# The first adaLN modulation computed feature tile by feature tile, with the first input projection k-outer inside it

## Chip, cores and metric

One core of one Trainium2 chip runs the kernel. The metric is the device time of one execution in microseconds (us); of several executions the median is given.

## What is computed

The reference runs two layers of a trunk on two groups of tokens, 512 latent tokens and 128 context tokens, with shared weights and 1024 features. Each layer modulates a normalised input, projects it to 8208 columns that feed three mixers and their gates, merges the branches, and ends with an MLP:

```python
mod_ctx = (jax.nn.silu(c_ctx) @ w_mod[l] + b_mod[l])[None, None, :]
mod_lat = (jax.nn.silu(c) @ w_mod[l] + b_mod[l])[:, None, :]
...
sh1, sc1, g1, sh2, sc2, g2 = jnp.split(mod, 6, axis=-1)
h = rmsnorm(x, lp['norm1']) * (1 + sc1) + sh1
proj = h @ lp['w_in'] + lp['b_in']
(da_q, da_k, da_v, ml_q, ml_k, ml_v, ml_o, ml_g,
 na_q, na_k, na_v, merge) = jnp.split(proj, np.cumsum(SPLIT_SIZES)[:-1].tolist(), axis=-1)
...
x = x + g1 * (merged @ lp['w_out'])
h2 = rmsnorm(x, lp['norm2']) * (1 + sc2) + sh2
u = jnp.square(jax.nn.relu(h2 @ lp['w_ff1'] + lp['b_ff1']))
x = x + g2 * (u @ lp['w_ff2'] + lp['b_ff2'])
```

The change lies in the first layer's `h` and the first two blocks of its `proj`: the columns `ml_v`, and the 16 gate columns `ml_g`.

## The kernel before

All 640 tokens stay on the chip, with features on the partitions: eight feature tiles `xT[k]` of 128 features by 640 tokens. Every float32 product is made of three float32r products, so each weight block and each activation is split into a rounded part `hi` and a rest `lo` (`split`, lines 215 to 218: ScalarE casts, VectorE subtracts). A weight block is 1 MB: 1024 features by 256 columns. `w_raw` asks for it on SP's queue (line 141), and there are two buffers. `gemm_b` (lines 200 to 213) makes 128 tokens by 256 columns: eight feature tiles times three matmuls, on lines 210, 211 and 212, which accumulate in one PSUM bank. `unit_b` does this for the five token tiles `t`; a unit's first step asks for the next unit's weights.

`start` (lines 1604 to 1664) is what comes ahead of the first unit. It asks for the eight feature tiles of x, sums their squares over the features (lines 1619 and 1621, then a matmul with ones, line 1636), takes 1/rms on GpSimd (line 1639), spreads it over the partitions with diagonal matrices and ones (lines 1643 and 1644), and multiplies it into x (line 1646). In between, `mod_first` (lines 278 to 299) computes the shift and scale of the first modulation, 2048 columns for the two conditioning vectors `cc3`. The 8 MB of weights `w_mod0` lie by input feature: tile k holds 128 input features by all 2048 columns. So each of the eight tiles adds to one PSUM bank, and the result exists only after the last tile. Four matmuls on line 287 write two rows each at partitions 0, 32, 64 and 96:

```python
for q in range(4):
    nc.tensor.matmul(ps[32 * q:32 * q + 2, :], self.cc3[:, :, k], raw[:, q * 512:(q + 1) * 512],
                     start=(k == 0), stop=(k == KD - 1))
```

Then the rows are copied (lines 291 and 292), transposed (line 295), added to the bias columns (line 299) and turned into a scale `A` and a shift `B` for each feature. Lines 1658 and 1660 apply them by token bank, (0, 256) and (256, 640), and split the result into the activations. The first unit's `gemm_b` follows: columns `ml_v` 0 to 255 with the 16 gate columns, 272 in all. Its evacuations (lines 604 and 610) feed the gate chain `ml_gates`, whose first step on TensorE is a transpose for each token tile (line 667). The second unit takes columns 256 to 511.

The order of instructions on each engine is set by a scheduling layer under the kernel's code, which moves an instruction ahead of others when it sees its inputs ready. What runs is that order, engine by engine, with semaphores; an engine executes its own instructions strictly one after the other.

Of the kernel before, what the change touches and what calls it, by code (L numbers as in the profile page):

```python
# [11 lines left out]
F32 = mybir.dt.float32  # L12
F32R = mybir.dt.float32r
AF = mybir.ActivationFunctionType
# [5 lines left out]
P = 128  # L20
# [5 lines left out]
TT = 5  # L26
# [60 lines left out]
class Builder:  # L87
# [190 lines left out]
    def mod_first(self, after):  # L278

        nc, I = self.nc, self.I  # L280
        ps = self.mm_ps()
        nc.vector.memset(ps, 0.0)
        for k in range(KD):
            raw = self.T(self.xp, [P, 2048], F32, "raw8", 6)
            nc.sync.dma_start(raw, I["w_mod0"][k])
            for q in range(4):
                nc.tensor.matmul(ps[32 * q:32 * q + 2, :], self.cc3[:, :, k], raw[:, q * 512:(q + 1) * 512],
                                 start=(k == 0), stop=(k == KD - 1))
            after(k)
        row = self.T(self.xp, [P, 512], F32, "modrow", 1)  # L290
        nc.vector.tensor_copy(row[:, :256], ps[:, :256])
        nc.scalar.copy(row[:, 256:], ps[:, 256:])
        tp = self.mm_ps()
        for j in range(4):
            nc.tensor.transpose(tp[:, j * P:(j + 1) * P], row[:, j * P:(j + 1) * P], self.ident)
        t4 = tp.rearrange("p (j q z) -> p j q z", j=4, q=4)
        jq = lambda x: x.rearrange("p (q j) -> p j q", q=4)
        for v in range(2):
            nc.vector.tensor_tensor(jq(self.modc[0][:, v, 0:16]), t4[:, :, :, v], jq(self.colv[0][1][:, 0:16]), op=ALU.add)

# [133 lines left out]
    def unit_b(self, c0, consume, extra=None):  # L434

        def prep():
            return self.w_bmode(self.in_blk(self.l, c0), extra=extra)

        def run(w):
            for t in range(TT):  # L440
                consume(t, self.gemm_b(w, self.act, t))
                yield
        return prep, run, None
# [1160 lines left out]
    def start(self):  # L1604

        tc, nc, I = self.tc, self.nc, self.I
        with tc.tile_pool(name="xp_in", bufs=1, reuse_waits="tile") as xp:
            self.xp = xp
            loads, fin = self.load_cols(0)
            self.xsrc = [I["x_sample"][0, t * P:(t + 1) * P] for t in range(4)] + [I["x_prompt"][0]]  # L1610
            xT = [self.hd() for _ in range(KD)]
            ws = []
            ones = self.T(xp, [P, P], F32, "ones", 1)
            nc.gpsimd.memset(ones, 1.0)
            acc = self.T(xp, [P, NT], F32, "acc", 1)
            for k in range(KD):
                nc.sync.dma_start(xT[k], I["xT"][:, k])
                sq = acc if k == 0 else self.T(xp, [P, NT], F32, "sq", 2)
                nc.scalar.activation(sq, xT[k], AF.Square)
                if k:  # L1620
                    nc.vector.tensor_tensor(acc, acc, sq, op=ALU.add)

            def after(k):
                if k == 1:
                    for o, i in loads:
                        nc.sync.dma_start(o, i)
                    fin()
                    normalize()
                if k == 4:
                    ws.append(self.first_w_in(0)())  # L1630

            def normalize():

                ps = self.t_ps()
                for t in range(TT):
                    nc.tensor.matmul(ps[:, 2 * t:2 * t + 2], acc[:, t * P:(t + 1) * P], ones[:, :2], start=True, stop=True)
                ss, r = self.st(5), self.st(5)
                nc.vector.tensor_scalar(ss, ps[:, 0:2 * TT:2], 1.0 / D, EPS, op0=ALU.mult, op1=ALU.add)
                nc.gpsimd.tensor_tensor(r, ss, self.mhalf[:, :TT], op=ALU.pow)
                rb = self.s_ps()  # L1640
                for t in range(TT):
                    dg = self.T(xp, [P, P], F32, "diag", 2)
                    nc.vector.tensor_scalar_mul(dg, self.ident, r[:, t:t + 1])
                    nc.tensor.matmul(rb[:, t * P:(t + 1) * P], ones, dg, start=True, stop=True)
                for k in range(KD):
                    nc.vector.tensor_tensor(xT[k], xT[k], rb[:, :NT], op=ALU.mult)
            self.mod_first(after)
            w, = ws
            A, B = self.mod_norm_cols(0, 0)
            act = [(self.act_slice(), self.act_slice()) for _ in range(KD)]  # L1650
            for a, b in BANKS:
                for k in range(KD):
                    x = xT[k]
                    for v, c0, c1 in ((0, a, min(b, NS)), (1, max(a, NS), b)):
                        if c0 >= c1:
                            continue
                        if a > 0 and v == 0 or a == 0 and k % 3 == 1:
                            nc.scalar.activation(x[:, c0:c1], x[:, c0:c1], AF.Identity, scale=A[:, v, k:k + 1], bias=B[:, v, k:k + 1])
                        else:
                            nc.vector.tensor_scalar(x[:, c0:c1], x[:, c0:c1], A[:, v, k:k + 1], B[:, v, k:k + 1],  # L1660
                                                    op0=ALU.mult, op1=ALU.add)
# [125 lines left out]
```

## Time and profile before

| what | us |
|---|---|
| median of 3 runs | 2491.88 |
| lowest and highest run | 2488.35 and 2492.19 |
| the profiled execution, its own time | 2490.52 |
| its span in the profile | 2488.7 |
| TensorE matmuls, busy | 2415.0 |
| VectorE, ScalarE, GpSimd, busy | 1523.0, 905.1, 640.9 |

The profiled execution is one run more, recorded by the hardware. Its span is 1.8 us shorter than its own time, which holds the launch as well. All times inside the trace count from the span's start. Busy shares are averages over the whole program; the stretch that the change touches is the first 60 us of it.

### The profile page before, as it was taken

The numbers are of one execution on the slowest core, as the hardware profiler recorded it, in microseconds if no ns is written. First come the engines' busy times: TensorE is split into PE (matmuls) and PEld (weight loads), VectorE is DVE, ScalarE is ACT, GpSimd is POOL, SyncE is SP. The second block draws the span as 40 slices with busy tenths as digits, with TensorE's granted clock in tenths as the row PEclk, the third lists the DMA queues.
The fourth block names the chain that finished last, engine by engine and source line by source line (L and its number), as shares of the span: only waits on it lengthen the run. The fifth ranks groups of instructions, "written<-read, shape, count | busy, mean of one in ns | idle before, by whom it ended". The sixth has DMA issues, their size and how long they took to land. (4 is left out here: it accounts for less than half of the span.)

```text
span 2488.7 us, 39544 instructions
## 1 busy us (share of the span) xinstructions
PE 2415.0 (97%) x15776; PEld 2266.3 (91%) x15776; DVE 1523.0 (61%) x2804; ACT 905.1 (36%) x1954; POOL 640.9 (26%) x701
## 2 busy tenths in 40 slices
PE   6999999999999999999999999999999999999998
PEld 4999999999998898999989999999989889999997
DVE  5557788566634899998565547674443464444444
ACT  4332354334433422223353334443443353322232
POOL 0122122233412233332021212222352312233301
PEclk8999999999999999999999999999999999999999
DMA  7323323333353334444332222223232722222221
GB/s 271 105 94 117 112 97 135 121 117 123 139 190 130 119 136 152 153 136 153 103 122 97 96 90 87 76 82 111 74 116 86 261 85 85 68 85 68 85 68 60
DMA packets 73706, 286.52 MB, mean 115 GB/s; under 512 B 9889, under 2 KB 21249, under 8 KB 49969
## 3 DMA queue, kind: packets, MB, share of 16 engines
q1 hardware_dynamic: 73520, 283.99, 33.3%
q8 instruction: 124, 2.03, 0.3%
q14 instruction: 62, 0.50, 0.1%
HBM read 257.60 MB, written 26.35 MB: 114 GB/s over the span
## 5 line engine op out<-in xcount | busy, mean ns | idle before, releaser
L191 PE MATMUL mm<-act,whi 128*128 128x384 f32 (+1 forms) x2176 | 699.4, 321 | 11.7 <-DVE act L503 3.4
L192 PE MATMUL mm<-act,whi 128*128 128x384 f32 (+1 forms) x2176 | 687.5, 316 | 0.0
L193 PE MATMUL mm<-act,wlo 128*128 128x384 f32 (+1 forms) x2176 | 686.0, 315 | 0.0
L217 ACT CAST whi<-raw 128x1024 fp32r<-128x1024 f32 x296 | 310.9, 1050 | 921.3 <-PE mm L192 439.3
L218 DVE TENSOR_TENSOR wlo<-raw,whi 128x1024 fp32r<-128x1024 f32 x296 | 383.8, 1297 | 381.3 <-ACT whi L217 327.2
L191 PEld LDWEIGHTS mm<-act,whi 128*128 128x128 f32 x2176 | 413.9, 190 | 17.5 <-issue 6.0
L192 PEld LDWEIGHTS mm<-act,whi 128*128 128x128 f32 x2176 | 414.3, 190 | 0.0
L193 PEld LDWEIGHTS mm<-act,wlo 128*128 128x128 f32 x2176 | 413.8, 190 | 0.0
L1535 POOL TENSOR_TENSOR x<-x,tmp 128x512 f32<-128x512 f32 x120 | 194.0, 1623 | 448.5 <-DVE tmp L1534 448.5
L210 PE MATMUL mm<-whi,act 128*128 128x256 f32 (+2 forms) x800 | 270.0, 338 | 0.0
L212 PE MATMUL mm<-whi,act 128*128 128x256 f32 (+2 forms) x800 | 267.1, 334 | 0.0
L211 PE MATMUL mm<-wlo,act 128*128 128x256 f32 (+2 forms) x800 | 266.4, 333 | 0.0
L323 DVE SCALAR_TENSOR_TENSOR macc<-raw,cc,macc 128x512 f32<-128x512 f32 x280 | 232.2, 874 | 20.0 <-DMA raw<-w_mod 19.6
L212 PEld LDWEIGHTS mm<-whi,act 128*128 128x128 f32 x800 | 152.0, 190 | 14.3
L211 PEld LDWEIGHTS mm<-wlo,act 128*128 128x128 f32 x800 | 152.1, 190 | 14.0
L210 PEld LDWEIGHTS mm<-whi,act 128*128 128x128 f32 x800 | 152.1, 190 | 14.0
L210 PE MATMUL t<-whi,act 128*128 128x512 f32 (+1 forms) x416 | 158.5, 381 | 1.7 <-ACT act L217 1.5
L211 PE MATMUL t<-wlo,act 128*128 128x512 f32 (+1 forms) x416 | 157.8, 379 | 0.0
L212 PE MATMUL t<-whi,act 128*128 128x512 f32 (+1 forms) x416 | 157.8, 379 | 0.0
L192 PE MATMUL t<-act,whi 128*128 128x256 f32 (+1 forms) x512 | 146.4, 286 | 0.0
L193 PE MATMUL t<-act,wlo 128*128 128x256 f32 (+1 forms) x512 | 146.4, 286 | 0.0
L191 PE MATMUL t<-act,whi 128*128 128x256 f32 (+1 forms) x512 | 146.2, 286 | 0.0
(286 smaller groups left out, 4168.6 us busy)
## 6 DMA issues: line engine op xcount, KB each, us to landing
raw<-w_in SPq DMA_DIRECT2D x64, 1024.0 KB
raw<-w_ff SPq DMA_DIRECT2D x64, 1024.0 KB
raw<-w_mod SPq DMA_DIRECT2D x48, 1024.0 KB
mgd<-act SPq DMA_DIRECT2D x32, 320.0 KB
act<-mgd SPq DMA_DIRECT2D x32, 320.0 KB
raw<-w_out SPq DMA_DIRECT2D x8, 1024.0 KB
gr<-gd SPq DMA_DIRECT2D x12, 512.0 KB
act<-rd SPq DMA_DIRECT2D x16, 320.0 KB
```

Of the source, the lines that this page charges most:

```text
L191: nc.tensor.matmul(o, wh, ah, start=(k == 0), stop=False)
L192: nc.tensor.matmul(o, wh, al, start=False, stop=False)
L193: nc.tensor.matmul(o, wl, ah, start=False, stop=(k == nk - 1))
L210: nc.tensor.matmul(o, ah, wh, start=(first and k == 0), stop=False)
L211: nc.tensor.matmul(o, ah, wlo, start=False, stop=False)
L212: nc.tensor.matmul(o, al, wh, start=False, stop=(last and k == nk - 1))
L217: self.nc.scalar.copy(hi, src)
L218: self.nc.vector.tensor_tensor(lo, src, hi.bitcast(F32), op=ALU.subtract)
L323: nc.vector.scalar_tensor_tensor(acc[v], r3[:, k, :], s, acc[v], op0=ALU.mult, op1=ALU.add)
L1535: nc.gpsimd.tensor_tensor(xs[t][:, sl], xs[t][:, sl], tmp, op=ALU.add)
```

## The change

`w_mod0` is laid out by output feature instead: tile j holds all 1024 input features for the shift and the scale of the 128 features of tile j. One tile is therefore enough for `A` and `B` of one feature tile. `mod_products(j)` (line 1632 of the new file) makes them with eight matmuls of 256 columns; for k and k + 4 they add up in one group of partitions, and the four groups hold partial sums. ScalarE copies the rows (line 1634), and two matmuls with a constant `sel` (line 1665, called the selector pair below) add the four partial sums and turn the rows into columns. `mod_apply(j)` makes `A` and `B` (lines 1666 and 1668), applies the scale together with 1/rms, which was spread to `rb` before (line 1650), in one three-operand pass on VectorE (line 1673), adds the shift in ScalarE's rounding pass (line 1674) and subtracts in another three-operand pass (line 1676). `project(j)` makes the first unit's matmuls of feature tile j for all five token tiles, into five PSUM banks, so that `unit_b` only evacuates. The request for the second block stands in `start` as well. On ScalarE the casts of the first weight block now stand behind the first activation of the second feature tile. The order of SP's requests changes: the first weight block comes after the second modulation tile instead of after the fifth.

The removed lines of `start` and `mod_first` are those printed above and are left out here.

```diff
@@ -275,29 +275,6 @@
         return (hb if half else cv)[:, i:i + 1]
 
 
-    def mod_first(self, after):
...
-        row = self.T(self.xp, [P, 512], F32, "modrow", 1)
...
@@ -434,11 +411,15 @@
     def unit_b(self, c0, consume, extra=None):
 
         def prep():
+            if self.raw_next is not None and extra is None:
+                raw, self.raw_next = self.raw_next, None
+                return self.w_bmode_split(raw)
             return self.w_bmode(self.in_blk(self.l, c0), extra=extra)
 
         def run(w):
+            sums, w = w if isinstance(w, tuple) else (None, w)
             for t in range(TT):
-                consume(t, self.gemm_b(w, self.act, t))
+                consume(t, self.gemm_b(w, self.act, t) if sums is None else sums[t])
                 yield
         return prep, run, None
 
@@ -1603,65 +1584,113 @@
 
     def start(self):
 
+
         tc, nc, I = self.tc, self.nc, self.I
         with tc.tile_pool(name="xp_in", bufs=1, reuse_waits="tile") as xp:
             self.xp = xp
+            self.order(xp, [("modrow", [P, 256], F32, 2), ("rb", [P, NT], F32, 1), ("raw8", [P, 2048], F32, 6)])
             loads, fin = self.load_cols(0)
             self.xsrc = [I["x_sample"][0, t * P:(t + 1) * P] for t in range(4)] + [I["x_prompt"][0]]
             xT = [self.hd() for _ in range(KD)]
...
             ones = self.T(xp, [P, P], F32, "ones", 1)
             nc.gpsimd.memset(ones, 1.0)
+            sel = self.T(xp, [P, 2], F32, "sel", 1)
+            nc.vector.tensor_reduce(sel, self.ident.rearrange("p (q z) -> p z q", q=4)[:, 0:2], axis=AX.X, op=ALU.add)
             acc = self.T(xp, [P, NT], F32, "acc", 1)
+            raws = []
+
+            def load_mod(j):
+                raw = self.T(xp, [P, 2048], F32, "raw8", 6)
+                raws.append(raw.rearrange("p (k c) -> p k c", k=KD))
+                nc.sync.dma_start(raws[j], I["w_mod0"][j])
             for k in range(KD):
                 nc.sync.dma_start(xT[k], I["xT"][:, k])
                 sq = acc if k == 0 else self.T(xp, [P, NT], F32, "sq", 2)
                 nc.scalar.activation(sq, xT[k], AF.Square)
                 if k:
                     nc.vector.tensor_tensor(acc, acc, sq, op=ALU.add)
...
+            load_mod(0)
+            for o, i in loads:
+                nc.sync.dma_start(o, i)
+            load_mod(1)
+            wraw = self.w_raw(self.in_blk(0, ML_V))
+            rx = self.T(self.wp, [P, 8, 16], F32, "rx", 1)
+            nc.sync.dma_start(rx, I["w_g"][0])
+            for j in range(2, KD):
+                load_mod(j)
+            self.raw_next = self.w_raw(self.in_blk(0, ML_V + 256))
+
+            mrow = self.s_ps()[:, :512]
+            nc.vector.memset(mrow, 0.0)
+            rows = []
+
+            def mod_products(j):
+
+                o = mrow[:, (j % 2) * 256:(j % 2) * 256 + 256]
+                for k in range(KD):
+                    q = k % 4
+                    nc.tensor.matmul(o[32 * q:32 * q + 2], self.cc3[:, :, k], raws[j][:, k], start=(k < 4), stop=(k >= 4))
+                rows.append(self.T(xp, [P, 256], F32, "modrow", 2))
+                nc.scalar.copy(rows[j], o)
+
+
+            ps = self.t_ps()
+            for t in range(TT):
+                nc.tensor.matmul(ps[:, 2 * t:2 * t + 2], acc[:, t * P:(t + 1) * P], ones[:, :2], start=True, stop=True)
+            mod_products(0)
+            ss, r = self.st(5), self.st(5)
+            nc.vector.tensor_scalar(ss, ps[:, 0:2 * TT:2], 1.0 / D, EPS, op0=ALU.mult, op1=ALU.add)
+            nc.gpsimd.tensor_tensor(r, ss, self.mhalf[:, :TT], op=ALU.pow)
+            rbp = self.s_ps()
+            for t in range(TT):
+                dg = self.T(xp, [P, P], F32, "diag", 5)
+                nc.vector.tensor_scalar_mul(dg, self.ident, r[:, t:t + 1])
+                nc.tensor.matmul(rbp[:, t * P:(t + 1) * P], ones, dg, start=True, stop=True)
+            rb = self.T(xp, [P, NT], F32, "rb", 1)
+            nc.scalar.copy(rb, rbp[:, :NT])
+            w = self.w_bmode_split(wraw, rx)
+            fin()
+            cv, cv2, _ = self.colv[0]
+            sc1 = self.T(self.cst, [P, KD], F32, "sc1", 1)
+            nc.gpsimd.tensor_scalar(sc1, cv2[:, 8:16], 1.0, None, op0=ALU.add)
+            cols = self.t_ps()
+            A = self.T(self.cst, [P, 2, KD], F32, "modA", 2)
+            B = self.modc[0][:, :, 0:8]
+            act = [(self.act_slice(), self.act_slice()) for _ in range(KD)]
+
+            def mod_apply(j):
+
+                c = cols[:, 4 * j:4 * j + 4]
+                for g in range(2):
+                    nc.tensor.matmul(c[:, 2 * g:2 * g + 2], rows[j][:, g * P:(g + 1) * P], sel, start=True, stop=True)
+                nc.vector.tensor_scalar(A[:, :, j], c[:, 2:4], sc1[:, j:j + 1], cv[:, ROW_N1 + j:ROW_N1 + j + 1],
+                                        op0=ALU.add, op1=ALU.mult)
+                nc.vector.tensor_scalar(B[:, :, j], c[:, 0:2], cv2[:, j:j + 1], None, op0=ALU.add)
+                x = xT[j]
+                hi, lo = act[j]
+                parts = ((0, 0, 256), (0, 256, NS), (1, NS, NT)) if j == KD - 1 else ((0, 0, NS), (1, NS, NT))
+                for v, a, b in parts:
+                    nc.vector.scalar_tensor_tensor(x[:, a:b], x[:, a:b], A[:, v, j:j + 1], rb[:, a:b], op0=ALU.mult, op1=ALU.mult)
+                    nc.scalar.activation(hi[:, a:b], x[:, a:b], AF.Identity, bias=B[:, v, j:j + 1])
+                for v, a, b in parts:
+                    nc.vector.scalar_tensor_tensor(lo[:, a:b], x[:, a:b], B[:, v, j:j + 1], hi[:, a:b].bitcast(F32),
+                                                   op0=ALU.add, op1=ALU.subtract)
+
+            s2 = self.s_ps()
+            sums = [o[:, :272] for o in (self.mm_ps(), self.mm_ps(), self.t_ps(), s2[:, :512], s2[:, 512:])]
+
+            def project(j):
                 for t in range(TT):
...
+                    self.gemm_b([w[j]], [act[j]], t, sums[t], first=(j == 0), last=(j == KD - 1))
+            mod_apply(0)
+            for j in range(1, KD):
+                mod_products(j)
+                if j >= 2:
+                    project(j - 2)
+                mod_apply(j)
+            project(KD - 2)
+            project(KD - 1)
+        return act, (sums, w)
 
     def run(self):
         tc, nc, I = self.tc, self.nc, self.I
@@ -1744,7 +1773,7 @@
         "w_out": halves(x["w_out"]),
         "w_ff2": halves(x["w_ff2"]),
         "w_mod": x["w_mod"].reshape(L, 2, 4, P, 12, 512).transpose(0, 4, 1, 3, 2, 5),
-        "w_mod0": x["w_mod"][0, :, :2048].reshape(KD, P, 2048),
+        "w_mod0": x["w_mod"][0, :, :2048].reshape(KD, P, 2, KD, P).transpose(3, 1, 0, 2, 4).reshape(KD, P, KD, 2 * P),
         "xT": xs.T.reshape(KD, P, NT).transpose(1, 0, 2),
         "x_sample": x["x_sample"],
         "x_prompt": x["x_prompt"],
```

What the scheduling layer made of it is seen at three places. In the names, `act` are feature tiles or their split parts, `raw` loaded weights, `whi` and `wlo` a block's two parts, `mm`, `t` and `s` PSUM tiles.

The first place is TensorE in the loop over feature tiles. Before, the last modulation tiles come one after the other, then the transposes of the row, then the projection, of which the first two token tiles alternate:

```order
L287 MATMUL mm_143<-raw_52_236,cc_89 2x512 x4
L287 MATMUL mm_143<-raw_53_242,cc_89 2x512 x4
L295 MATMUL mm_251<-ident_78,modrow_248 128x128 x4
L210 MATMUL t_373<-whi_218,act_260 128x272
L211 MATMUL t_373<-wlo_219,act_260 128x272
L210 MATMUL mm_420<-whi_218,act_260 128x272
```

And now, from the fifth modulation tile's products (`raw_38`) to the sixth's (`raw_39`), around the matmuls of the fourth feature tile (`mm_248` and `mm_249` are the sums of token tiles 0 and 1):

```order
L1632 MATMUL s_43_172<-raw_38_162,cc_89 2x256 x8
L210 MATMUL mm_248<-whi_212,act_237 128x272
L211 MATMUL mm_248<-wlo_213,act_237 128x272
L212 MATMUL mm_248<-whi_212,act_238 128x272
L210 MATMUL mm_249<-whi_212,act_237 128x272
L1665 MATMUL t_229<-sel_115,modrow_359 128x2 x2
L211 MATMUL mm_249<-wlo_213,act_237 128x272
...
L212 MATMUL s_80_247<-whi_212,act_238 128x272
L1632 MATMUL s_43_172<-raw_39_164,cc_89 2x256 x8
```

Each tile's products now stand between the matmuls of two feature tiles, and its selector pair stands behind four of them.

The second place is VectorE where the first unit's sums are evacuated (lines 604 and 610, now 585 and 591). Before, the evacuation of the first two token tiles comes ahead of the split of the next weight block:

```order
L604 TENSOR_TENSOR act_354<-t_373,gb_352 128x2x2x4
L610 TENSOR_TENSOR v_356<-t_373,vb_350 128x2x128
...
L218 TENSOR_TENSOR wlo_403<-raw_400,whi_402 128x1024
L218 TENSOR_TENSOR act_275<-act_109,act_274 128x384
L218 TENSOR_TENSOR wlo_407<-raw_400,whi_406 128x1024
```

Now:

```order
L1673 SCALAR_TENSOR_TENSOR act_112<-act_112,modA_230,rb_210 128x128
L1676 SCALAR_TENSOR_TENSOR act_246<-act_112,modc_226,act_245 128x256 x2
L1676 SCALAR_TENSOR_TENSOR act_246<-act_112,modc_226,act_245 128x128
L218 TENSOR_TENSOR wlo_568<-raw_170,whi_567 128x1024
L218 TENSOR_TENSOR wlo_572<-raw_170,whi_571 128x1024
L585 TENSOR_TENSOR act_546<-mm_248,gb_544 128x2x2x4
L591 TENSOR_TENSOR v_548<-mm_248,vb_542 128x2x128
```

All five evacuations now follow the split of the next block, where two of them came ahead of it.

The third place is VectorE in the gate chain, some 20 us later (lines 693 to 709, now 674 to 690). Before, no weight split stands in it:

```order
L693 COPY st_589<-st_588 36x3
L694 COPY st_589<-st_414 4x1
L695 COPY st_589<-st_588 4x3
L701 TENSOR_TENSOR act_605<-act_583,st_589 36x640
L706 COPY st_590<-act_605 36x5
L709 TENSOR_TENSOR act_613<-act_605,st_589 36x640
```

Now:

```order
L674 COPY st_654<-st_653 36x3
L218 TENSOR_TENSOR wlo_828<-raw_825,whi_827 128x1024
L675 COPY st_654<-st_579 4x1
L676 COPY st_654<-st_653 4x3
L591 TENSOR_TENSOR v_556<-mm_772,vb_542 128x2x128
L682 TENSOR_TENSOR act_670<-act_648,st_654 36x640
L218 TENSOR_TENSOR wlo_832<-raw_825,whi_831 128x1024
L687 COPY st_655<-act_670 36x5
L690 TENSOR_TENSOR act_678<-act_670,st_654 36x640
```

Both subtractions of a later block's split have moved into the chain.

## Rows read from the trace of the kernel before

**Rows 1.** The profile's page, part 1: busy time, share and instructions of each engine.
```profile
PE 2415.0 (97%) x15776; PEld 2266.3 (91%) x15776; DVE 1523.0 (61%) x2804; ACT 905.1 (36%) x1954; POOL 640.9 (26%) x701
```

**Rows 2.** TensorE before the projection, timeline: start, length, engine, line, idle before.
```profile
13.59 2.27 PE L1636 MATMUL t<-ones,acc 128*128 128x2 f32 x10 [13.59 <-DVE acc L1621]
...
18.94 1.89 PE L287 MATMUL mm<-raw,cc 128*2 128x512 f32 x8
...
22.66 4.05 PE L287 MATMUL mm<-raw,cc 128*2 128x512 f32 x32
...
29.52 1.06 PE L287 MATMUL mm<-raw,cc 128*2 128x512 f32 x8 [2.81 <-DMA raw<-w_mod]
...
34.52 1.89 PE L287 MATMUL mm<-raw,cc 128*2 128x512 f32 x8 [0.61 <-DMA raw<-w_mod]
```

**Rows 3.** Busy time by stretch of 2 us; PEclk is the granted clock.
```profile
30.00:32.00 2.00, 0.58 (x8) 0.00 (x0) 1.41 (x4) 0.00 (x0) 0.10 (x1) 0.60 1.01 418
...
42.00:44.00 2.00, 2.00 (x11) 2.00 (x10) 2.00 (x7) 2.00 (x6) 0.00 (x0) 0.50 1.00 410
44.00:46.00 2.00, 2.00 (x18) 2.00 (x17) 2.00 (x7) 2.00 (x6) 0.00 (x0) 0.98 0.60 178
```

**Rows 4.** TensorE in the first unit and at its end, timeline.
```profile
39.63 0.59 PE L210 MATMUL t<-whi,act 128*128 128x272 f32 x1 [1.50 <-ACT act L217]
...
53.76 0.28 PE L212 MATMUL t<-whi,act 128*128 128x272 f32 x1
...
54.89 0.29 PE L210 MATMUL t<-whi,act 128*128 128x272 f32 x1
...
56.77 0.60 PE L667 MATMUL s<-ident,act 128*100 128x128 f32 x4
```

**Rows 5.** Durations: L323, L218 by line (ns min/median/max), L630 by form (mean), others timeline.
```profile
L323 DVE SCALAR_TENSOR_TENSOR macc<-raw,cc,macc x280: 726/744/2882, 153.2 to 1187.3; 128x512 f32<-128x512 f32 x140
...
L218 DVE TENSOR_TENSOR wlo<-raw,whi x296: 1206/1224/3248, 28.8 to 2456.2; 128x1024 fp32r<-128x1024 f32 x148
...
L630 ACT ACTIVATE act<-mm,colv 128x384 f32<-128x384 f32 x8 | 4.6, 575 | 0.0
L630 ACT ACTIVATE act<-mm,colv 128x256 f32<-128x256 f32 x8 | 3.8, 474 | 8.4 <-PE mm L193 8.3
...
58.26 0.70 ACT L670 COPY act<-s 36x640 f32<-36x640 f32 x1 [0.23 <-PE s L667]
...
36.93 0.37 ACT L292 COPY modrow<-mm 128x256 f32<-128x256 f32 x1 [7.77 <-DVE modrow L291]
...
26.88 1.04 ACT L217 CAST whi<-raw 128x1024 fp32r<-128x1024 f32 x1 [14.52 <-DMA raw<-w_in]
```

**Rows 6.** SP's queue and the first load's first use, timeline.
```profile
1.17 4.09 SPq L1617 DMA_DIRECT2D act<-xT  x8
...
4.50 0.74 ACT L1619 ACTIVATE acc<-act 128x640 f32<-128x640 f32 x1 [1.84 <-DMA act<-xT]
...
24.58 0.42 SPq L141 DMA_DIRECT2D raw<-w_in  x1
...
36.46 0.83 SPq L1354 DMA_DIRECT2D mlm<-k_mlm  x2
```

**Rows 7.** TensorE and ScalarE behind the second unit, timeline.
```profile
72.73 0.36 PE L191 MATMUL mm<-act,whi 128*128 128x256 f32 x1 [0.73 <-DVE st L693]
...
76.92 0.44 PE L191 MATMUL mm<-act,whi 128*128 128x384 f32 x1 [1.08 <-DVE v L610]
...
78.62 0.74 ACT L721 ACTIVATE act<-act 36x640 f32<-36x640 f32 x1
...
81.19 1.02 PE L729 MATMUL t<-ident,act 100*128 100x100 f32 x10
```

**Rows 8.** The change from broadcasts to products on TensorE, timeline.
```profile
17.79 1.22 PE L1644 MATMUL s<-diag,ones 128*128 128x128 f32 x4 [1.93 <-DVE diag L1643]
...
18.94 0.11 PEld L287 LDWEIGHTS mm<-raw,cc 128*2 128x2 f32 x8 [0.22 <-issue]
```

More of the change, by code (lines that the diff above doesn't have):

```diff
@@ L275, in bin_col @@
         return (hb if half else cv)[:, i:i + 1]
-    def mod_first(self, after):
[L280 to L289, printed above, removed]
-        row = self.T(self.xp, [P, 512], F32, "modrow", 1)
[L291 to L299, printed above, removed]
     def mod_store(self, l, n, src):
@@ L1611, in start @@
             xT = [self.hd() for _ in range(KD)]
-            ws = []
             ones = self.T(xp, [P, P], F32, "ones", 1)
             nc.gpsimd.memset(ones, 1.0)
+            sel = self.T(xp, [P, 2], F32, "sel", 1)
+            nc.vector.tensor_reduce(sel, self.ident.rearrange("p (q z) -> p z q", q=4)[:, 0:2], axis=AX.X, op=ALU.add)
             acc = self.T(xp, [P, NT], F32, "acc", 1)
+            raws = []
[3 more added lines that the diff above has]
+                nc.sync.dma_start(raws[j], I["w_mod0"][j])
             for k in range(KD):
@@ L1621, in start @@
                     nc.vector.tensor_tensor(acc, acc, sq, op=ALU.add)
[L1623 to L1634, printed above, removed]
-                for t in range(TT):
[L1636 to L1661, printed above, removed]
-                    hi, lo = act[k]
-                    self.split(hi[:, a:b], lo[:, a:b], x[:, a:b])
@@ L1664, in start @@
-        return act, w
+            load_mod(0)
[10 more added lines that the diff above has]
+            nc.vector.memset(mrow, 0.0)
```

## Prediction

> **What bounds the kernel now.** I read the page's busy shares first: TensorE is busy for 2415.0 of 2488.7 us [rows 1]. Time is saved only by handing TensorE its work earlier or by making that work shorter, and the stretch that the change rewrites is the only long thin one.
>
> Next the order of time on TensorE. The last three modulation tiles arrive 2.5 us apart, the first of them at 29.52 and the last at 34.52; a tile's products take 1.06 us at the full clock and 1.89 at half, and in between TensorE waits for the loads [rows 2]. After the last one comes a serial chain (row copied, transposed, made into columns, first activations), and the first projection starts at 39.63. It then runs without a gap to 56.77, where the gate transposes stand [rows 4]. So there is room: from 29.52 to 39.63 TensorE has some 6 us of work.
>
> Third the granted clock. It falls inside 30 to 32 us, after that thin stretch, to 0.50, which is 1.2 GHz instead of 2.4; eleven matmuls fit into 42 to 44 us, and eighteen into 44 to 46, when it is back [rows 3], some 4.2 us after unbroken work began at 39.63. At the full level the 272-column matmuls start 0.1256 us apart (53.76 to 54.89, nine steps [rows 4]). The first tile's products, at 18.94, took 1.89 us, so TensorE is at its lower rate there too, and at the full one from 22.66 on, where sixteen matmuls took 4.05 us [rows 2].
>
> **What is removed and added.** Gone are eight 640-column passes that multiplied x by 1/rms, the scale-and-bias passes by bank and the transposes of the row. For each feature tile there come, on VectorE, two column sums, a three-operand pass over 640 columns and a three-operand subtraction; on ScalarE a row copy and a biased pass; on TensorE a selector pair. A 128x512 three-operand pass is 0.744 us in the median; a biased ScalarE pass is 0.474 us for 256 columns and 0.575 for 384, so about 0.68 for 512 [rows 5]. VectorE's chain is then some 2.6 us a tile, with ScalarE's pass inside it, which is under TensorE's pace below. The request of the next block "there too" I cost at nothing: the queue issues it at 24.58 us already [rows 6].
>
> **Start of the new projection.** The norm's broadcasts end at about 22.3 (products follow them at 22.66 [rows 2], and two waits for buffers go). Then, in the order in which the instructions now stand: 1/rms copied, 0.70; x pass of tile 0, 0.74; its two activations, 0.68 and 0.37; row copy of tile 1, 0.37; selector pair, 0.5; two column sums, 0.3; x pass of tile 1, 0.74; its activation, 0.68; and only then ScalarE's casts of the weight block, 1.04, and an estimated 0.2 for the 64 gate columns [rows 5]. That is 6.3 us, at about 28.6; the block itself has landed by 26.9 even in the old order [rows 5]. TensorE issues four matmuls and waits for VectorE's subtraction of the weights, 1.22 us [rows 5], until 29.9. The projection starts ten microseconds earlier than at 39.63.
>
> **What paces it.** From 29.9 TensorE has to issue 116 of the block's 120 matmuls, at 0.1256: 14.6 us. Six more modulation tiles: eight matmuls of 256 columns in two groups of four stream what four of 512 did, 1.01 each (4.05 / 4 [rows 2]), 6.1 us. Six selector pairs, each loading 128x128 float32 weights for two columns: five such matmuls took 2.27 us at the low rate, 0.45 each [rows 2], and five transposes 1.02 at the high one, 0.20 each [rows 7]; I take 0.28, near the full-clock row, 3.4 us, with 2.4 and 5.4 as ends. Ahead of each pair TensorE waits for ScalarE's row copy, 0.37 and signals less the four matmuls put in between, about 0.25: 1.5 us. The sum is 25.6 us, at 55.5. That is 3.7 us a tile against loads every 2.5. **TensorE paces this loop, not the loads**: the last tile has landed by about 34.5, and its products come near 49.
>
> **The clock.** From about 23.8 to 29.9 TensorE does one selector pair and four matmuls. A stretch like it (26.7 to 32 with one tile's products) ended at 0.50 [rows 2, 3], so I expect the same near 28 and 4.2 us of unbroken work before it is back. Half of that is 2.1, of which the loop's waits swallow some: 1.7. Ends: 0 if the clock holds, 3.4 if the return takes twice as long. The first block ends at 57.2.
>
> **The tail.** After the last selector pair VectorE has two column sums (0.3), three x passes (0.45, 0.45, 0.3), three subtractions as long, both 1.22 us subtractions of the next weight block, for the first of which it waits for ScalarE, and only then, by its order, the first evacuation (0.4): 5.5 us. TensorE has 3.3 us of matmuls left there. The gate transposes stand at the head of its queue, so it waits 2.2 us, to 59.5. That is 2.7 us **later** than 56.77 [rows 4]. All that was gained ahead is given back, because the block now shares TensorE with the modulation at that pace and its evacuations come at one time, behind the next split.
>
> **After that** the second block is unchanged, and the two waits behind it (0.73 and 1.08 us [rows 7]) keep their size. One thing moves: two weight subtractions (2.4 us) now stand inside VectorE's gate chain, whose result TensorE transposes. It came without a wait at 81.19, ScalarE's last input ending at 79.36 [rows 7], a slack of 1.8; now it waits about 1.0 us (2.4 less 1.8, and 0.4 for the casts ahead of ScalarE's pass). Ends 0 and 1.2. Beyond, TensorE's work is the same and a delay passes through.
>
> SP's queue: the mask loads waited for the last tile's products (issued at 36.46 [rows 6]), and they wait for those again, to about 52; the bias rows stand behind them and go out near 54. A load at the start took 3.3 us from issue to first use (1.17 to 4.50 [rows 6]), so they land near 57.5. VectorE asks for them at 59: covered.
>
> **The sum:** 2.7 + 1.0 = +3.7 us on the profiled execution's 2490.52 us: **2494 us**. That execution lies 1.4 below the median of the three runs, 2491.88. No change is what lies within 0.2%, 5.0 us, about what a measurement of this kernel can tell. Ends: with the clock held (-1.7), no wait in the gate chain (-1.0) and cheap selectors (-1.0), 0; with each at its dear end (+1.7, +0.2, +2.0), +7.6.
>
> **The rivals.**
> *Changes between narrow and full-width matmuls cost time (slower).* The products write two columns in four column groups, the projection uses the whole array, and the loop goes over from one to the other twelve times. The row that speaks of it: behind the broadcasts the products' weight loads stand idle for 0.22 us for no shown reason, while the matmul rows abut (17.79 + 1.22 is past 18.94) [rows 2, 8]. So 0 to 0.22 a change, 0 to 2.6 in all; I take 0, by the matmul rows. From 0.11 a change the total passes 5.0; at 0.22 it is +6.3, 2496.8. The Trainium skill (TensorEngine Tiling (Array Packing), Key Properties) says that going over to another tiling mode drains TensorE; by it this rival holds, and the rows bear it out as that idle 0.22 at most.
>
> *The lower clock holds through the loop (slower).* If small products and waits keep it from coming back, about 100 matmuls cost 0.11 us more, the products 5.2 and the pairs 2.0: +2.0 without the old clock term, +18 with it, together +20, 2510; for half the loop +11, 2502. Against it: from 22.66 products alone ran at the full rate [rows 2].
>
> *The bias rows land late (slower).* Beyond 59 each microsecond costs one. Landing at 60.5 would add 1.5: 2495.7. It decides from 60.3.
>
> *The loads pace the loop (faster).* If a tile took TensorE under 2.5 us, the block would end near 40, and the second begin near 41, behind its split: 16 us earlier, 2475. It would need products and pair in 0.6 us beside 15 matmuls (1.9); the rows give 1.3 and more.
>
> That the change doesn't do what it says is so for one part, the earlier request of the next block.
>
> **How the numbers follow.** Forecast 0.57, changes of width 0.25, lower clock 0.08, late bias rows 0.05, loads pace 0.05. So slower 0.38, same 0.57, faster 0.05. The range begins at 2489, the sum's low end less 1.5 for the spread of the runs (2488.35 to 2492.19), and reaches to 2502, which takes in the dear ends, the width changes, the late rows and half of the lower clock. Left out are the faster rival and the full lower clock, 0.1 together, and some of the unknown.
>
> **What would show it.** Right: the first 128x272 matmul near 28.6; products 3.5 to 4 us apart, up to about 49, none waiting for its load from the third tile on; a granted clock of 0.5 for some 4 us around 30; a wait of some 2 us ahead of the gate transposes, released by VectorE, to 59.5. Wrong: a first block done before 50, or products spaced by their loads, where the price of products or pairs failed. Gaps of 0.1 to 0.2 us on both sides of each group of products speak for the first rival, a granted clock of 0.5 beyond 36 us for the second.

## The result, and the profile after

The changed kernel takes 2510.91 us, the median of four runs (2509.05 to 2515.64); the kernel before takes 2490.33 beside it, also of four (2488.35 to 2492.19). The ratio is 1.0088, interval 1.0076 to 1.0100: slower by 20.6 us, where 3.7 was forecast and the range ended at 2502. The profiled execution is the slowest of the four, 2515.64, with a span of 2513.9.

The page's busy line answers to [rows 1]. TensorE is busy 15.3 us longer, and 9.9 us more of the span is not busy time:

```profile
PE 2430.3 (97%) x15868; PEld 2280.5 (91%) x15868; DVE 1527.3 (61%) x2814; ACT 906.3 (36%) x1952; POOL 641.4 (26%) x702
```

First the stretch that the change rewrites, TensorE's timeline, which answers to [rows 2, 4, 8]:

```profile
18.64 1.22 PE L1648 MATMUL s<-diag,ones 128*128 128x128 f32 x4 [3.09 <-DVE diag L1647]
...
23.83 1.89 PE L1632 MATMUL s<-raw,cc 128*2 128x256 f32 x16
26.51 1.01 PE L1665 MATMUL t<-sel,modrow 128*128 128x2 f32 x4 [0.80 <-ACT modrow L1634]
30.52 0.82 PE L210 MATMUL mm<-whi,act 128*128 128x272 f32 x2 [2.99 <-ACT whi L217]
...
38.10 0.29 PE L211 MATMUL s<-wlo,act 128*128 128x272 f32 x1
38.31 1.05 PE L1632 MATMUL s<-raw,cc 128*2 128x256 f32 x16
39.29 0.39 PE L212 MATMUL s<-whi,act 128*128 128x272 f32 x1
39.52 0.29 PE L210 MATMUL mm<-whi,act 128*128 128x272 f32 x1
...
39.91 0.61 PE L1665 MATMUL t<-sel,modrow 128*128 128x2 f32 x4
40.38 0.37 PE L210 MATMUL mm<-whi,act 128*128 128x272 f32 x1
40.59 0.29 PE L211 MATMUL mm<-wlo,act 128*128 128x272 f32 x1
...
49.28 1.05 PE L1632 MATMUL s<-raw,cc 128*2 128x256 f32 x16
...
52.91 1.05 PE L1632 MATMUL s<-raw,cc 128*2 128x256 f32 x16
...
58.39 0.29 PE L212 MATMUL s<-whi,act 128*128 128x272 f32 x1
60.75 0.29 PE L648 MATMUL s<-ident,act 128*100 128x128 f32 x1 [2.07 <-DVE act L585]
```

The projection starts at 30.52, the products come without a wait for a load, those of the seventh tile at 49.28 and of the eighth and last at 52.91, and the gate transposes wait 2.07 us for VectorE, to 60.75, 3.98 later than 56.77 [rows 4]. This is the forecast's picture with a somewhat dearer sum. So I set the starts of the same matmul in both traces against each other:

| place | before | changed | later by |
|---|---|---|---|
| gate transposes | 56.77 | 60.75 | 3.98 |
| in the gate chain | 84.10 | 90.64 | 6.54 |
| behind the mixers' first part | 165.03 | 168.12 | 3.09 |
| end of the first layer's mixers | 740.14 | 744.22 | 4.08 |
| feed-forward part, first layer | 872.71 | 876.79 | 4.08 |
| | 896.82 | 904.81 | 7.99 |
| | 945.93 | 959.44 | 13.51 |
| | 1006.51 | 1025.05 | 18.54 |
| | 1066.92 | 1089.09 | 22.17 |
| | 1127.42 | 1153.15 | 25.73 |
| its end | 1188.00 | 1215.79 | 27.79 |
| end of the program | 2470.93 | 2496.32 | 25.39 |

At 872.71 the delay is 4.08, close to the forecast's 3.7. This is one pair of executions: the last matmul of the first layer's mixers stands at 740.14, 738.86, 737.61 and 737.46 in four traces that run the old kernel's instructions up to there (before, e9, e2, e5 below), and at 744.22, 744.04, 742.07 and 741.41 in four that run the changed ones (after, e1, e8, e3); the means lie 4.4 apart. Then 23.7 us are lost in six steps, 800 us behind the last line that the change touches. TensorE's waits from 850 to 1260 us (engine and line, what it waited for, us in all, times, longest), of the kernel before:

```profile
PE t L330 <- DVE tmp L1534: 0.8, 1, 0.8
```

and of the changed kernel:

```profile
PE t L307 <- DVE tmp L1515: 8.0, 6, 2.7
PE t L191 <- DVE st L308: 5.9, 6, 1.1
```

Here is one of the six steps on TensorE, in the changed kernel:

```profile
942.58 0.28 PE L193 MATMUL mm<-act,wlo 128*128 128x256 f32 x1
942.70 0.60 PE L307 MATMUL t<-ident,macc 128*128 128x128 f32 x4
946.04 0.82 PE L307 MATMUL t<-ident,macc 128*128 128x128 f32 x4 [2.74 <-DVE tmp L1515]
946.51 0.56 PE L191 MATMUL mm<-act,whi 128*128 128x256 f32 x1
...
948.25 0.69 PE L191 MATMUL t<-act,whi 128*128 128x384 f32 x1 [0.54 <-DVE st L308]
```

on VectorE there:

```profile
940.62 0.68 DVE L1515 TENSOR_TENSOR tmp<-t,gr 128x512 f32<-128x512 f32 x1
941.22 2.43 DVE L300 SCALAR_TENSOR_TENSOR macc<-raw,cc,macc 128x512 f32<-128x512 f32 x2
943.57 0.68 DVE L1515 TENSOR_TENSOR tmp<-mm,gr 128x512 f32<-128x512 f32 x1
944.17 1.21 DVE L218 TENSOR_TENSOR wlo<-raw,whi 128x1024 fp32r<-128x1024 f32 x1
945.30 0.68 DVE L1515 TENSOR_TENSOR tmp<-t,gr 128x512 f32<-128x512 f32 x1
945.90 1.70 DVE L218 TENSOR_TENSOR wlo<-raw,whi 128x1024 fp32r<-128x1024 f32 x1
947.52 0.68 DVE L308 TENSOR_REDUCE st<-t 128x4 f32<-128x512 f32 x1
```

and the same step in the kernel before, with two rows of VectorE behind those of TensorE:

```profile
934.58 0.28 PE L193 MATMUL t<-act,wlo 128*128 128x256 f32 x1
935.68 0.66 PE L330 MATMUL t<-ident,macc 128*128 128x128 f32 x4 [0.82 <-DVE tmp L1534]
936.09 0.42 PE L191 MATMUL mm<-act,whi 128*128 128x384 f32 x1
936.35 0.60 PE L330 MATMUL t<-ident,macc 128*128 128x128 f32 x4
...
934.95 0.68 DVE L1534 TENSOR_TENSOR tmp<-t,gr 128x512 f32<-128x512 f32 x1
...
936.68 0.68 DVE L1534 TENSOR_TENSOR tmp<-mm,gr 128x512 f32<-128x512 f32 x1
```

The difference is in the names: `mm` and `t` have changed places. The background work of the feed-forward part is the next layer's modulation, whose chunks (`mod_chunk_dve`) end with two groups of transposes, each into a PSUM tile of pool `t`, which has two. VectorE evacuates the 512-column sums of the feed-forward block ahead of them on line 1534, now 1515. Before, the last of these sums lies in `mm`, and the second group starts at 936.35, ahead of that evacuation (936.68). Now it lies in `t`, the second group waits until VectorE has evacuated it (945.30 + 0.68), and the 384-column sum behind, now in `t` too, waits for the first group's reduction (947.52 + 0.68).

Who changed that? `mm_ps` (line 106) flips `self.alt` at each call and, in the feed-forward phase, takes `t` at every other one. Before, `start` called it twice (lines 281 and 293) and the first unit five times, once for each token tile; now `start` calls it twice for its five sums (line 1680) and the first unit not at all. Five calls fewer is odd: from there on every sum of the feed-forward parts has the other pool.

The waits cost more than their length, because the granted clock falls behind most of them. The windows of the changed kernel (stretch, its length, busy time of PE, PEld, DVE, ACT, POOL, granted clock, DMA):

```profile
944.00:946.00 2.00, 0.00 (x0) 0.00 (x0) 2.00 (x4) 0.00 (x0) 1.67 (x1) 1.00 0.56 143
946.00:948.00 2.00, 1.68 (x8) 1.39 (x8) 2.00 (x2) 0.00 (x0) 2.00 (x2) 0.60 0.90 381
948.00:950.00 2.00, 1.75 (x5) 1.75 (x6) 2.00 (x6) 0.00 (x0) 0.72 (x1) 0.50 0.71 152
950.00:952.00 2.00, 2.00 (x8) 2.00 (x8) 2.00 (x5) 0.00 (x0) 0.00 (x0) 0.50 0.88 373
952.00:954.00 2.00, 2.00 (x10) 2.00 (x9) 2.00 (x4) 0.00 (x0) 0.00 (x0) 0.70 0.03 8
```

In this step the granted clock is down to 0.50, half the rate (1.2 GHz), for most of seven microseconds. Of the 23.7 us, 13.9 are waits. The other 9.8 come within some 8 us behind the waits; the record shows the clock fall in five of the six steps (none behind the last, from 1192.65), and its mean from 850 to 1260 us is 0.98, against 1.00 in the kernel before.

### The profile page after: what moved, and what is told of

It is laid out like the page before. It is cut to its first block, busy times and chain, and to the rows that moved or that the text cites. A ratio compares the mean times of both kernels' runs of the same rounds, so it can differ in the third digit from the quotient of the medians.

```text
span 2513.9 us, 39744 instructions
## 1 busy us (share of the span) xinstructions
PE 2430.3 (97%) x15868; PEld 2280.5 (91%) x15868; DVE 1527.3 (61%) x2814; ACT 906.3 (36%) x1952; POOL 641.4 (26%) x702
## 4 chain that ended last, share of the span: by engine, by line
PE 72%; DVE 10%; issue 4%; DMA 3%; POOL 3%; ACT 1%; SPq 0%; POOLq 0%; DVEq 0%
PE mm L191 11%; PE mm L192 11%; PE mm L193 11%; PE mm L212 4%; PE mm L211 4%; PE mm L210 4%; PE t L191 4%; PE t L192 3%; PE t L193 3%; DVE macc L300 3%; PE t L212 2%; PE t L211 2%; PE t L210 2%; DVE wlo L218 2%; DMA raw<-w_mod 2%
## 5 line engine op out<-in xcount | busy, mean ns | idle before, releaser
L191 PE MATMUL mm<-act,whi 128*128 128x256 f32 (+1 forms) x2176 | 675.7, 311 | 11.4 <-DVE act L484 3.4
L192 PE MATMUL mm<-act,whi 128*128 128x256 f32 (+1 forms) x2176 | 663.3, 305 | 0.0
L193 PE MATMUL mm<-act,wlo 128*128 128x256 f32 (+1 forms) x2176 | 662.7, 305 | 0.0
L218 DVE TENSOR_TENSOR wlo<-raw,whi 128x1024 fp32r<-128x1024 f32 x296 | 384.7, 1300 | 402.8 <-ACT whi L217 347.8
L210 PE MATMUL mm<-whi,act 128*128 128x256 f32 (+2 forms) x808 | 273.7, 339 | 3.1 <-ACT whi L217 3.0
L212 PE MATMUL mm<-whi,act 128*128 128x256 f32 (+2 forms) x808 | 270.5, 335 | 0.0
L300 DVE SCALAR_TENSOR_TENSOR macc<-raw,cc,macc 128x512 f32<-128x512 f32 x280 | 230.6, 868 | 16.8 <-DMA raw<-w_mod 16.6
L191 PE MATMUL t<-act,whi 128*128 128x384 f32 (+1 forms) x512 | 174.3, 341 | 5.9 <-DVE st L308 5.9
L192 PE MATMUL t<-act,whi 128*128 128x384 f32 (+1 forms) x512 | 173.1, 338 | 0.0
L193 PE MATMUL t<-act,wlo 128*128 128x384 f32 (+1 forms) x512 | 172.8, 338 | 0.0
L210 PE MATMUL t<-whi,act 128*128 128x512 f32 (+1 forms) x392 | 150.5, 384 | 0.0
L211 PE MATMUL t<-wlo,act 128*128 128x512 f32 (+1 forms) x392 | 150.5, 384 | 0.0
L212 PE MATMUL t<-whi,act 128*128 128x512 f32 (+1 forms) x392 | 150.5, 384 | 0.0
```

The costliest lines, as they stand in the source:

```text
L191: nc.tensor.matmul(o, wh, ah, start=(k == 0), stop=False)
L192: nc.tensor.matmul(o, wh, al, start=False, stop=False)
L193: nc.tensor.matmul(o, wl, ah, start=False, stop=(k == nk - 1))
L210: nc.tensor.matmul(o, ah, wh, start=(first and k == 0), stop=False)
L211: nc.tensor.matmul(o, ah, wlo, start=False, stop=False)
L212: nc.tensor.matmul(o, al, wh, start=False, stop=(last and k == nk - 1))
```

## The experiments

**Theory (the turn):** the odd number of calls is the whole of the loss beyond 4 us. **Rival (the shift alone):** being 4 us late moves VectorE's passes against TensorE in the feed-forward part, whatever the banks. Two runs tell them apart.

**e1, only the turn put back.**

```diff
             project(KD - 1)
+        self.alt = not self.alt
         return act, (sums, w)
```

> The changed kernel with one statement more at the end of start: self.alt is flipped once, so that mm_ps alternates in the feed-forward parts as it did before the change. Theory of the turn: the change calls mm_ps twice ahead of the mixers where the old kernel called it seven times, an odd difference, so in the feed-forward part of the first layer every sum lies in the other of the two PSUM pools, and the transposes of the modulation chunk, which take both buffers of pool t, find one still held. Then TensorE's 13.9 us of waits on lines 307 and 191 between 850 and 1250 us go, with the half-rate stretches behind them; what stays is the 4.07 us by which the changed kernel is behind at 765 us: 2494.4 us, 2492 to 2497. Rival, the shift alone: being some 4 us late moves VectorE's passes against TensorE in the feed-forward part, whatever the banks: the time stays at 2511, 2508 to 2514.

Measured: 2489.44 us (11 runs), the kernel before 2487.95 (15 runs), ratio 1.0009 (1.0000 to 1.0018). The twelve waits are gone, one of 0.9 is left:

```profile
PE t L307 <- DVE tmp L1515: 0.9, 1, 0.9
```

The rival falls. Of the 20.6 us some 19 were the turn: the ratio goes from 1.0088 to 1.0009. The time lies under the theory's own range too, so its other half, that the 4.07 us stay, missed. In e1's trace the same matmuls stand 6.61 us later than in the kernel before at 84.10, 3.88 at 765.08, 4.25 at 1250.08, 2.12 at 1399.90 and 0.55 at 2470.93; by the medians 1.5 us are left at the end.

**e2, the kernel before with only the turn changed.**

```diff
+            if l == 0:
+                self.alt = not self.alt
             self.xs, gr = [], {}
```

> The kernel before with one flip of self.alt at the start of the first layer's feed-forward part, nothing else. Theory of the turn: it loses what the changed kernel loses there: 20.6 us of the medians less the 4.1 that the changed kernel is behind at 765 us, 16.5 us: 2507, 2504 to 2513, with waits of TensorE behind the transposes of line 330 and behind the reduction on line 331. Rival, the shift alone: no change, 2490, 2488 to 2493.

Measured: 2509.25 (5 runs), ratio 1.0094 (1.0079 to 1.0108). One flip in an otherwise untouched kernel costs 21.3 us by the medians, about the same:

```profile
PE t L330 <- DVE tmp L1536: 7.6, 6, 2.7
PE t L191 <- DVE st L331: 6.5, 6, 1.1
```

**e3 and e5, another bank for the transposes**, in the changed kernel and in the one before.

```diff
+        tps = self.s_ps() if self.ff_phase else None
         for v in range(2):
-            tp = self.t_ps()
+            tp = self.t_ps() if tps is None else tps[:, v * 512:(v + 1) * 512]
```

> The changed kernel, the turn left as it is, but in the feed-forward phase the two groups of transposes of a modulation chunk go to one double bank of pool s2 instead of to two buffers of pool t. Theory of the turn, mechanism two transposes groups against two t buffers that hold sums: the waits on lines 307 and 191 go although the turn is the wrong one: about the same as with the turn restored, 2494.4, 2492 to 2498. Rival, VectorE itself is late with its sums and reductions: the wait moves to the next sum that needs a buffer, 2508 to 2513.

> The kernel before with the transposes of a modulation chunk in pool s2 in the feed-forward phase. By the theory of the turn little is to be had, since its turn leaves pool t free: its waits on line 330 in all are 1.8 us, so 2488.5 to 2490.5. If the chunk's banks cost it time that the waits don't show (sums held back by the two buffers), more: under 2487.

Measured: 2515.31 (4 runs), 1.0115 (1.0098 to 1.0131), and 2512.29 (5 runs), 1.0100 (1.0085 to 1.0115). Both missed. The row of e3 says why:

```profile
PE s L308 <- DVE st L309: 16.7, 6, 4.3
```

The two groups shared one tile, and the second now waited for the reduction of the first: the edit had made a new wait of the old kind, in the kernel before as well (16.6 us in six places).

**e8 and e9, the same with a tile for each group.**

```diff
-            tp = self.t_ps()
+            tp = self.s_ps()[:, :512] if self.ff_phase else self.t_ps()
```

> The changed kernel, turn as it is; in the feed-forward phase each of the two groups of transposes of a modulation chunk gets a double bank of pool s2 of its own (in e3 both shared one, and the second group waited for the reduction of the first, 16.7 us in six waits). Mechanism of the turn, two groups that need both buffers of pool t while a sum still holds one: the six waits on line 307 and the six on line 191 behind the reductions go, without touching the turn: as with the turn restored, 2491, 2488 to 2495. Rival, VectorE is late there whatever the banks: 2505 or more.

> The kernel before with the same two double banks of pool s2. Its turn leaves pool t free there, one wait of 0.8 us in all between 850 and 1260 us: no change, 2486 to 2490 beside 2488. If the banks themselves cost something (transposes placed earlier on TensorE's queue, with nothing left to hold them back), some us slower.

Measured: 2489.20 (11 runs), 1.0002 (0.9993 to 1.0011), and 2487.28 (11 runs), 1.0000 (0.9991 to 1.0008), beside 2488.07 (33 runs) for the kernel before. TensorE has no wait listed from 850 to 1260 us in either. With the wrong turn kept, the loss is gone: it was the two buffers of `t`, not VectorE's lateness.

**e6, e7, e11, the 4 us that are left.** They ask whether the loop ends earlier when it starts earlier, as it must if TensorE paces it. All have the turn put back. Their expectations call the products at 49.3 those of the last tile; they are the seventh's, the eighth's come at 52.91 in the changed kernel and at 53.59 in e1. e6 puts the casts of the first block ahead of ScalarE's first row copy:

```diff
-            mod_products(0)
+            w = self.w_bmode_split(wraw, rx)
+            with tc.issue_after(self.last_cast.ins):
+                mod_products(0)
```

> The turn restored as in e1, and the casts of the first weight block put ahead of ScalarE's first row copy, so that the block is split near 24 us instead of 32.9. Theory that TensorE paces the loop: the first projection starts near 26.5 instead of 30.5 and the whole loop ends some 3.5 us earlier; but the casts of the next block then stand ahead of the last tile's activations, 2 us against it; gate transposes at 57 to 59 instead of 60.8, the whole 2486 to 2489 beside 2489.4. Rival, the loop is paced by something else (row copies, loads): first projection earlier, products of the last tile still at 49.3, no change.

Measured: 2491.11 (11 runs), 1.0016 (1.0007 to 1.0026); no gain. The first projection came at 29.50, not 26.5 (30.46 in e1): the row copy now stood behind the casts, and the first selector pair waited for it:

```profile
26.52 0.98 PE L1666 MATMUL t<-sel,modrow 128*128 128x2 f32 x4 [3.23 <-ACT modrow L1634]
```

The loop's last matmul came 1.2 us earlier than in e1, but the first evacuation now stood behind three weight subtractions on VectorE, the wait ahead of the gate transposes grew from 2.08 to 2.96, and they came at 61.07 (61.42 in e1).

e7 adds the next block's split inside the loop:

```diff
+                if j == 5:
+                    self.raw_next = self.w_bmode_split(self.raw_next)
...
+                    with tc.issue_after(self.last_cast.ins), tc.issue_after(self.last_sub.ins):
+                        mod_apply(j)
```

> As e6, and the next block's split put inside the loop ahead of the sixth tile's column sums, the bias rows requested ahead of the mask loads, and the split of the block after that behind the first block's evacuations. Theory: the tail wait of 2.07 us on the first gate transpose goes, and with the earlier start the gate transposes stand at 54.5 to 55.5, 6 us ahead of e1 and 1.5 to 2 ahead of the kernel before (56.77); the gate chain waits some 1 us less. The whole 2482 to 2486, if no later wait takes it back. Rival: waits with dates of their own further on take it back, as they did with 3 of e1's 3.9 us: 2487 to 2490.

Measured: 2493.28 (11 runs, 2487.70 to 2497.41), 1.0018 (1.0008 to 1.0027); a miss again. The eighth tile's products came at 47.05, but ScalarE ran the new casts only behind the eighth row copy, VectorE stood behind them, and TensorE with it:

```profile
52.30 1.01 PE L1672 MATMUL t<-sel,modrow 128*128 128x2 f32 x4 [4.21 <-DVE modc L1675]
```

The gate transposes came at 61.83, not 54.5 to 55.5. This shows why nothing was gained at the start, not why the medians of e6 and e7 lie above e1's: at 84.10 their traces are 5.84 and 5.87 us later than the kernel before, e1's 6.61, and e7's is of its fastest execution.

e11 sets both orders by hand: casts in halves behind the first row copy, the next split in halves behind the fourth and fifth tile.

```diff
+            with tc.issue_after(self.last_row.ins):
+                w = self.w_bmode_split(wraw, rx, (0,))
...
+                elif j in (4, 5):
+                    nxt += self.w_bmode_split(self.raw_next, None, (j - 4,))
+                    with tc.issue_after(self.last_cast.ins), tc.issue_after(self.last_sub.ins):
+                        step(j)
```

> What e7 wanted, with the orders that failed there mended (in e7 ScalarE's casts of the next block stood behind the eighth row copy, and TensorE waited 4.2 us for the column sums; the first casts stood ahead of the first row copy and held back the first selector pair by 3.2 us). As e1, and: the first block's casts behind the first row copy and around the copy of 1/rms; the next block split in two halves inside the loop, behind the fourth and the fifth tile; bias rows requested ahead of the mask loads; the split after that behind the first block's evacuations. Theory, TensorE paces the loop: first projection at 26.5 to 28 instead of 30.5, no wait ahead of the first gate transpose, which stands at 54.5 to 56.5 (e1: 61.4), ahead of the 56.77 of the kernel before. The whole: 0.9985 to 0.9995 of the kernel before if later waits keep what they took from e1, that is 3 of its 3.9 us; 0.997 to 0.998 if all of it is kept. Rival: the second half of the program has waits with dates of their own, nothing is gained: 0.9995 to 1.0010.

Measured: 2484.99 (11 runs), the kernel before 2489.22 (15 runs), 0.9985 (0.9976 to 0.9994), at the edge of what was expected, and the only version whose interval lies under 1. Its TensorE:

```profile
26.79 0.40 PE L210 MATMUL mm<-whi,act 128*128 128x272 f32 x1
...
56.12 0.27 PE L649 MATMUL s<-ident,act 128*100 128x128 f32 x1
```

The projection starts 3.7 us ahead of the changed kernel's, the wait ahead of the gate transposes is gone, and they stand at 56.12, 0.65 ahead of the kernel before. So the loop can be worth its place, once the weight splits are moved away from its end. Which of e11's four moves does it no run separates, and the start alone doesn't explain it: at 84.10 e11's trace is 0.19 behind the kernel before, and at 165.03 it is 3.32 ahead, by a stretch of waits in the mixers that is told below.

## Why the prediction was wrong

**The step that failed** is the sentence "Beyond, TensorE's work is the same and a delay passes through." The work is the same; where its sums lie is not. I costed the edit to `unit_b` ("so that it only evacuates") by its matmuls and evacuations, and did not count the calls of `mm_ps` that went with it, though seven and two can be counted from the two kernels, and the order of TensorE's instructions shows `mm` and `t` exchanged. No rival held it, and the range was made of local terms alone. The price shown is some 19 to 21 us (e1, e2; e8 shows the two buffers of `t` to be the cause). The second half of the sentence failed too, in the other direction: with the turn put back, 6.61 us at 84.10 are 1.5 us at the end (e1), so most of that delay does not pass through.

The Trainium skill (Perfetto Trace Analysis, Optimization Strategy) says that one gap repeating on the engine that should be saturated can mean that there is no SBUF or PSUM for the next tile. The trace agrees, with six waits behind line 1515 and six behind line 308.

**The start** was forecast at 28.6 and came at 30.52. The order was as I had it. The broadcasts through the diagonal matrices began 0.85 later than before (18.64 against 17.79) and ended at 23.26 instead of 22.3; the x pass of tile 0 waited for that tile's own column sums, some 0.4 that I had not counted; and the second tile's selector pair took 1.01 us, not 0.5 (26.51).

**The pace** held: from the fourth tile on products stand 3.6 to 3.8 us apart, forecast 3.7, none waits for its load, and TensorE shows no wait from 31 us to the block's end. The loop's last matmul ended near 58.6, forecast 57.2. "Up to about 49" for the last products was a slip of its own: behind them stand 30 matmuls and a pair, some 5.6 us with the products, so the sum itself put them near 51.6; they came at 52.91. Inside it two terms erred against each other. The row copies, 1.5 us in the sum, cost no wait in the steady loop. The changes of width cost about 0.1 us each: 0.21 from 38.10 to 38.31 and 0.23 from 39.29 to 39.52, in place of 0.1256. Twelve of them make 1.1 us; I had taken 0, with 0.22 each as the dear end. The Trainium skill (TensorEngine Tiling (Array Packing), Key Properties) says that going over to another tiling mode drains TensorE; the rows allow it 0.1 us at most. Behind a selector pair, which uses the whole array, the next two matmuls stand 0.21 apart as well (40.38 and 40.59), so it is not shown that the width is what costs it.

**The clock** was forecast to fall near 28. In this execution's record it never did before 62, yet only twelve matmuls fit into 32 to 34 us, half the rate. In e1, whose instructions up to there are the same, the record has it at 0.67 from 26 to 28 us, at 0.50 from 28 to 36 and at 0.77 to 38, with the same spacing of the matmuls. The last row below is e1's, the others are the changed kernel's:

```profile
32.00:34.00 2.00, 2.00 (x12) 1.74 (x16) 1.25 (x3) 0.00 (x0) 0.00 (x0) 1.00 1.03 430
...
62.00:64.00 2.00, 2.00 (x13) 2.00 (x12) 0.58 (x3) 0.19 (x1) 0.00 (x0) 0.58 0.80 324
64.00:66.00 2.00, 2.00 (x12) 2.00 (x12) 0.82 (x1) 1.97 (x3) 0.00 (x0) 0.56 0.88 293
...
32.00:34.00 2.00, 2.00 (x12) 1.67 (x15) 1.18 (x3) 0.00 (x0) 0.00 (x0) 0.50 1.01 422
```

So the fall came much as forecast; why one record lacks it no run shows. Until about 35.4 the matmuls are slow, 4.9 us of them: twelve at 0.1 us too much and one tile's products at 0.5, so the term of 1.7 was about right. A second fall, behind the tail's wait, was not in the sum; in this pair of traces it goes with 1.7 more (3.98 late at 56.77, 5.63 at 60.08), and e1's trace, which has the same wait, does not show it.

**The tail**: 2.07 us of wait, forecast 2.2, released by the first evacuation, which stands directly behind the two subtractions of the next split. **The gate chain**: TensorE waits 1.1 and 0.3 us on line 710, forecast 1.0. **SP**: the bias rows went out at 55.5 and 56.0 and were not waited for. **The request of the next block** went out at 26.16, where the old queue had it at 24.58; its worth by itself no run shows.

So the local terms add up to 6.54 at 84.10, not 3.7. Some 3.4 of it come back by 165, in a part of the mixers where TensorE waits in both kernels (from 130 us on, for the VectorE pass that writes `C`). Before, it is one wait of 3.5 us, and from 156 to 164 us the granted clock falls behind it (0.68, 0.50, 0.50, 0.62 in stretches of 2 us); in the changed kernel there are two, 2.1 us in all, and the clock stays at 1.00. The first row is the kernel before's, the other two are the changed one's:

```profile
158.12 0.80 PE L812 MATMUL t<-v,act 128*128 128x129 f32 x2 [3.46 <-DVE C L821]
...
161.85 0.49 PE L793 MATMUL t<-v,act 128*128 128x129 f32 x2 [1.02 <-DVE C L802]
...
165.60 0.49 PE L786 MATMUL t<-v,act 128*128 128x129 f32 x2 [1.12 <-DVE C L802]
```

That is why 4.08 looks like the forecast. This part was luck: I had no term for it.

## What to carry to other kernels

When an edit adds or removes calls to a helper that rotates buffers or alternates pools, count the calls: an odd difference moves every later buffer, and the price shows up wherever a queue happened to fit the old turn. Give short-lived scratch tiles of their own, one for each group that is written before the other is read (e3 against e8). And compare the built order, buffer names included, to the last instruction, not only around the edit.

## What was not expected of the hardware

The granted clock in the records and the pace of matmuls can differ: 1.00 in 32 to 34 us, while matmuls of 272 columns lay 0.227 us apart; from 35.4 on 0.1256, with the same 1.00. Another execution of the same instructions, e1's, has 0.50 in its record there. The spacing of equal matmuls is the surer reading.

A wait of TensorE can cost well over its length: twelve waits in six places, 13.9 us in all, took 23.7 us from the program, with a granted clock of 0.5 to 0.7 behind five of the six. It did not take a long stop: at 1131.52 and 1133.73 TensorE waited 0.64 and 1.08 us, and the clock stood at 0.50 from 1135 to 1137 us. Nor does every such stop bring it down, as the two waits of 1.0 and 1.1 us near 165 us show.

Executions of the same instructions wander apart by 1 to 3 us at a few places: at 740.14 us of the kernel before, e9, e2 and e5 are 1.3 to 2.7 us ahead of it. One pair of traces doesn't carry a difference below that.
